# The MLP's first product by Strassen's scheme in three of four quarters of a one-core decoder block

## The chip, the cores and the metric

The kernel runs on one core of one Trainium2 chip. The metric is the device time of one execution in microseconds; the kernel before is given by the median of three runs. A profile of one further execution shows what each engine did: TensorE (PE, and PEld for its weight loads), VectorE (DVE), ScalarE (ACT), GpSimd (POOL) and SyncE (SP), whose queue issues the loads of weights.

## The reference, cut to what matters

```
x  is (512 tokens, 1024), w_mlp_in (1024, 4096), w_mlp_out (4096, 1024), all float32
x  = x + rmsnorm(merged @ w_out, g_post_mix)
h  = rmsnorm(x, g_pre_mlp)
f  = square(relu(h @ w_mlp_in)) @ w_mlp_out
x  = x + rmsnorm(f, g_post_mlp)
x  = x + sigmoid(x @ w_ple_gate) * (p @ w_ple_proj)
```

Ahead of this stand the three mixers (convolution, differential attention, pooling) with their gates; the change touches none of that.

## The kernel before

Activations lie with features on the partitions and the 512 tokens in the columns: a tile of 128 features is 128x512. All weights lie in one array of 144 chunks, 128x1024 each, in the order in which they are used; one chunk is one output tile of a 1024-deep product (eight blocks of 128x128, one for each step kt of the depth).

Each product keeps about float32 precision with the type float32r: both operands are split into a high and a low part, and `mm3` (lines 153 to 156) issues three matmuls for each block: high by high, weight high by moving low, weight low by moving high. A full output tile is 8 steps by 3 matmuls of 512 columns into one of eight PSUM banks (tags mm and at, four each; `bank2` takes them in turn).

`Weights` feeds this. `load` (L76) issues a chunk's DMA on SP's queue into one of three raw buffers. `split` makes the two parts: a cast on ScalarE (L90) into wh, then a subtraction on VectorE (L94) into wl. The parts go to slots; from the end of the mixers on there are eight (pools hlp with three and hlp2 with five), and `get` keeps the splits that many chunks ahead. A raw buffer is free when its subtraction has run.

The MLP is done in four quarters of 1024 hidden features. In each, eight output tiles of the first product (`one_tile(xg)`; xg is x1 times its gain, split, not yet normalised) go through `hidden`: VectorE takes max(b, 0) times rB2 (x1's rstd, L898), ScalarE squares (L899), and `mul_split` (L149 on ScalarE, L150 on VectorE) splits into sh and sl. Eight tiles of the second product (`one_tile(s_hl)`) follow and are added up in f: by a copy on ScalarE in quarter 0 (L934), by an addition on VectorE in quarters 1 and 2 (L936). In quarter 0 the first four output tiles are done side by side and in token halves of 256 (`side_by_side_halves`). In quarter 3 the second product runs in `split_output`: four tiles side by side, then four tiles in token halves, with TensorE's order written out by hand; `evac_f` (L907) adds to f, sums the squares for the next rmsnorm (L832, L835, L836) and scales (L909). Between the halves TensorE computes the rstd of a half (`rstd_steps`: L211 sums over partitions, VectorE and GpSimd take the power, L216 broadcasts), and `residual_half` (L853, L854) and a split make x2 for the last product.

Except where TensorE's order is written out by hand, a planner orders each engine's instructions ahead of time: of those that it takes to be ready it picks the one written first. On the chip each engine then runs its list strictly in that order.

Of the kernel before, what the change touches and what calls it, by code (L numbers as in the profile page):

```python
# [9 lines left out]
F32 = mybir.dt.float32  # L10
F32R = mybir.dt.float32r
AF = mybir.ActivationFunctionType
ALU = mybir.AluOpType
# [19 lines left out]
N_RAW, N_SPLIT, N_ACT, N_LOGIT, N_NORM, N_QK = 3, 3, 32, 6, 3, 12  # L33
TCARGS = dict(schedule_with_timeline_sim=True)
P = 128
S = 512
HALF = 256
D = 1024
# [9 lines left out]
G_PRE_MIX, G_POST_MIX, G_PRE_MLP, G_POST_MLP = 0, 8, 16, 24  # L48
# [9 lines left out]
class Weights:  # L58
# [3 lines left out]
    def __init__(self, tc, wdram, raw_pool, hl_pool):  # L62
        self.tc, self.nc, self.w = tc, tc.nc, wdram
        self.raw_pool = raw_pool
        self.turns = [hl_pool] * N_SPLIT
        self.n = wdram.shape[0]
        self.loaded = self.done = 0
        self.limit, self.pin = self.n, False
        self.tiles, self.raw = {}, {}

    def load(self, i, halves=False):
        while self.loaded <= min(i, self.n - 1):
            c = self.loaded
            self.raw[c] = self.raw_pool.tile([P, 1024], F32, tag="raw", name=f"raw{c}")
            if not halves:
                self.nc.sync.dma_start(out=self.raw[c], in_=self.w[c])  # L76
            self.loaded += 1
# [3 lines left out]
        self.nc.sync.dma_start(out=self.raw[c][:, sl], in_=self.w[c][:, sl])  # L81

    def tiles_of(self, c):
        pool = self.turns[c % len(self.turns)]
        return [pool.tile([P, 1024], F32R, tag=t, name=f"{t}{c}") for t in ("wh", "wl")]

    def split(self, c, sl=slice(0, 1024), parts="hl"):
        src, (wh, wl) = self.raw[c][:, sl], self.tiles[c]
        if "h" in parts:
            i = self.nc.scalar.copy(out=wh[:, sl], in_=src)  # L90
            if self.pin:
                self.tc.keep_in_program_order(i)
        if "l" in parts:
            i = self.nc.vector.tensor_tensor(out=wl[:, sl], in0=src, in1=wh[:, sl].bitcast(F32), op=ALU.subtract)  # L94
            if self.pin:
                self.tc.keep_in_program_order(i)

    def upto(self, i):
        while self.done <= min(i, self.n - 1):
            c = self.done  # L100
            self.load(c)
            self.tiles[c] = self.tiles_of(c)
            self.split(c)
            self.done += 1

    def get(self, i):
        self.upto(max(i, min(i + len(self.turns) - 1, self.limit)))
        return self.tiles[i]


# [1 line left out]
def block_kernel(ctx: ExitStack, tc: tile.TileContext, xT, pT, wts, pool_w, par, rel_bias, onehot, out):  # L112
    nc = tc.nc
# [20 lines left out]
    def act_tile(name, dt=F32, tag=None, pool=None, n=S):  # L134
        uid[0] += 1
        tag = tag or OWN.get(name, "a")
        return (pool or ap).tile([P, n], dt, tag=tag, name=f"{name}_{uid[0]}", bufs=BUFS.get(tag))

    def bank(tag="mm"):
        uid[0] += 1  # L140
# [12 lines left out]
    def mm3(o, sh, sl, mh, ml, first, last):  # L153
        nc.tensor.matmul(out=o, lhsT=sh, rhs=mh, start=first, stop=False)  # L154
        nc.tensor.matmul(out=o, lhsT=sh, rhs=ml, start=False, stop=False)  # L155
        nc.tensor.matmul(out=o, lhsT=sl, rhs=mh, start=False, stop=last)  # L156
# [37 lines left out]
    def pcol(c, n=1):  # L194
        return par_sb[:, c:c + n]
# [10 lines left out]
    def rstd_steps(sq, lo, n, inv_n, got, tag="at"):  # L206


        b = bank(tag)
        for j in range(n):  # L210
            nc.tensor.matmul(out=b[:, j:j + 1], lhsT=sq[:, lo + j * P:lo + (j + 1) * P], rhs=ones_col,  # L211
                             start=True, stop=True)
        r = rstd_from(b[:, 0:n], inv_n, n, "pe")
        yield
        for j in range(n):
            nc.tensor.transpose(out=b[:, j * P:(j + 1) * P], in_=r[:, j:j + 1].to_broadcast([P, P]), identity=ident)  # L216
        got(b[:, 0:n * P])
# [49 lines left out]
    chunk = [0]  # L267
# [484 lines left out]
        norm_g = Stream(conv_norm())  # L752
    drain(norm_g)
    atp_ctx.close()
    hlp2 = ctx.enter_context(tc.tile_pool(name="hlp2", bufs=8 - N_SPLIT))
    W.turns = [hlp] * N_SPLIT + [hlp2] * (8 - N_SPLIT)
    mg = []
    for m in range(KT):
        add_branch(m, conv_gates[m], y_mm(m, c_hl))
# [16 lines left out]
    def bank2():  # L776
        turn2[0] += 1
        return bank(("mm", "at")[turn2[0] % 2])
# [23 lines left out]
    def split_output(src, evac, done):  # L802

        W.limit = chunk[0] + KT + 3
        cs = [next_chunk() for _ in range(N_SIDE)]
        bs = [bank2() for _ in range(N_SIDE)]
        for kt in range(KT):
            for (wh, wl), b in zip(cs, bs):
                mm3(b, wh[:, kt * P:(kt + 1) * P], wl[:, kt * P:(kt + 1) * P], *src[kt], kt == 0, kt == KT - 1)
        for m in range(N_SIDE):  # L810
            evac(m, bs[m], slice(0, S))
        cs = [next_chunk() for _ in range(KT - N_SIDE)]
        bs = [bank2() for _ in range(KT - N_SIDE)]
        paced = None
        with tc.manual_schedule(engines={mybir.EngineType.PE}):
            for hf in range(2):
                for m in range(KT - N_SIDE):
                    for kt in range(KT):
                        half_mm(bs[m], *cs[m], src, kt, HALVES[hf], paced)
                    evac(m + N_SIDE, bs[m], HALVES[hf])  # L820
                if paced:
                    paced.finish()
                else:
                    paced = Paced(done(0), PACE_OUT)
# [5 lines left out]
    def sum_squares(total, src, first, sl):  # L830
        if first:
            nc.scalar.activation(out=total[:, sl], in_=src, func=AF.Square)  # L832
        else:
            q = act_tile("sq")
            nc.scalar.activation(out=q[:, sl], in_=src, func=AF.Square)  # L835
            nc.vector.tensor_tensor(out=total[:, sl], in0=total[:, sl], in1=q[:, sl], op=ALU.add)  # L836
# [29 lines left out]
    split_output(mg, evac_mix, mix_done)  # L866


    def side_by_side_halves(src, done):
        cs = [next_chunk() for _ in range(4)]  # L870
        bs = [bank2() for _ in range(4)]
        paced = Paced(done(1), PACE_IN)
        with tc.manual_schedule(engines={mybir.EngineType.PE}):
            for sl in HALVES:
                for kt in range(KT):
                    for c, b in zip(cs, bs):
                        half_mm(b, *c, src, kt, sl, paced)
                    if paced.n >= PACE_IN[1] + PACE_IN[2] * KT and W.limit < W.n:
                        W.limit, W.pin = W.n, True
                        W.upto(min(chunk[0] + W_AHEAD, W.n - 1))  # L880
                        W.pin = False
        paced.finish()
        return bs

    def one_tile(src):
        wh, wl = next_chunk()
        b = bank2()
        for kt in range(KT):
            mm3(b, wh[:, kt * P:(kt + 1) * P], wl[:, kt * P:(kt + 1) * P], *src[kt], kt == 0, kt == KT - 1)
        return b  # L890

    f = [act_tile("f", tag=t) for t in spare]
    fsum = act_tile("fsum", tag="norm")
    rB2 = [None]

    def hidden(b):
        t = act_tile("t")
        nc.vector.scalar_tensor_tensor(out=t, in0=b, scalar=0.0, in1=rB2[0], op0=ALU.max, op1=ALU.mult)  # L898
        nc.scalar.activation(out=t, in_=t, func=AF.Square)  # L899
        hl = act_tile("sh", F32R), act_tile("sl", F32R)  # L900
        mul_split(*hl, t)
        return hl
# [2 lines left out]

    def evac_f(m, b, sl):
        nc.vector.tensor_tensor(out=f[m][:, sl], in0=f[m][:, sl], in1=b[:, sl], op=ALU.add)  # L907
        sum_squares(fsum, f[m][:, sl], m == 0, sl)
        nc.scalar.activation(out=f[m][:, sl], in_=f[m][:, sl], func=AF.Copy, scale=pcol(G_POST_MLP + m))  # L909

# [8 lines left out]
    for quarter in range(4):  # L919
        s_hl = []  # L920
        if quarter == 0:
            bs = side_by_side_halves(xg, mix_done)
            rB2[0] = act_tile("rB")
            for _ in rstd_steps(x1sum, 0, 4, 1.0 / D, lambda b: nc.scalar.copy(out=rB2[0], in_=b)):
                pass
            s_hl = [hidden(b) for b in bs]
            s_hl += [hidden(one_tile(xg)) for _ in range(4)]
        else:
            s_hl = [hidden(one_tile(xg)) for _ in range(8)]
        if quarter < 3:  # L930
            for m in range(KT):
                b = one_tile(s_hl)
                if quarter == 0:
                    nc.scalar.copy(out=f[m], in_=b)  # L934
                else:
                    nc.vector.tensor_tensor(out=f[m], in0=f[m], in1=b, op=ALU.add)  # L936
        else:
            split_output(s_hl, evac_f, f_done)


# [137 lines left out]
```

## Time and profile before

| | |
|---|---|
| median of three runs | 838.5 us (837.84 to 839.13) |
| the profiled execution | 838.38 us, of which the span from first to last instruction is 836.6 us |
| busy: PE, PEld, DVE, ACT | 829.7, 699.8, 504.7, 347.1 us |
| granted TensorE clock | 0.999 of full |

Busy times are sums over the whole span. A PE instruction's shown duration is longer than the distance to the next one, because matmuls overlap; the distance from start to start is what a matmul costs in a stream. Back-to-back instructions on DVE and ACT overlap by a little too.

### The profile page before, as it was taken

The numbers are of one execution on the slowest core, as the hardware profiler recorded it, in microseconds if no ns is written. First come the engines' busy times: TensorE is split into PE (matmuls) and PEld (weight loads), VectorE is DVE, ScalarE is ACT, GpSimd is POOL, SyncE is SP. The second block draws the span as 40 slices with busy tenths as digits, with TensorE's granted clock in tenths as the row PEclk, the third lists the DMA queues.
The fourth block names the chain that finished last, engine by engine and source line by source line (L and its number), as shares of the span: only waits on it lengthen the run. The fifth ranks groups of instructions, "written<-read, shape, count | busy, mean of one in ns | idle before, by whom it ended". The sixth has DMA issues, their size and how long they took to land.

```text
span 836.6 us, 10573 instructions
## 1 busy us (share of the span) xinstructions
PE 829.7 (99%) x4132; PEld 699.8 (84%) x4132; DVE 504.7 (60%) x832; ACT 347.1 (41%) x560; POOL 29.0 (3%) x66
## 2 busy tenths in 40 slices
PE   8999999999999999999999999999999999999998
PEld 6788888888888888888999888888888888889997
DVE  5869669965579985675377631443334434435672
ACT  6734635555452323752445542342233223425341
POOL 2200000010000000000000000000000000000000
PEclk9999999999999999999999999999999999999999
DMA  8463332222222232265303423322223222223311
GB/s 281 153 229 108 113 101 76 86 80 75 77 75 82 95 101 88 92 219 181 101 2 119 158 80 122 101 95 85 98 101 100 98 83 97 100 76 99 104 61 67
DMA packets 27522, 89.09 MB, mean 106 GB/s; under 512 B 3244, under 2 KB 3628, under 8 KB 27472
## 3 DMA queue, kind: packets, MB, share of 16 engines
q1 hardware_dynamic: 26160, 83.95, 29.9%
q0 software_dynamic: 1312, 4.47, 1.5%
q8 instruction: 32, 0.52, 0.3%
q14 instruction: 18, 0.15, 0.1%
HBM read 84.20 MB, written 5.52 MB: 107 GB/s over the span
## 4 chain that ended last, share of the span: by engine, by line
PE 96%; DVE 2%; DMA 1%; ACT 1%; issue 0%; SPq 0%; DVEq 0%; ACTq 0%
PE mm L156 21%; PE mm L154 21%; PE mm L155 21%; PE at L154 10%; PE at L155 10%; PE at L156 10%; PE at L211 1%; DMA raw<-in_wts_dram 1%; PE at L457 1%; PE at L455 1%; PE at L488 1%; DVE ssum L294 1%; PE at L216 0%; DVE wl L94 0%; ACT wh L90 0%
## 5 line engine op out<-in xcount | busy, mean ns | idle before, releaser
L90 ACT CAST wh<-raw 128x1024 fp32r<-128x1024 f32 (+1 forms) x144 | 148.8, 1038 | 337.1 <-PE mm L155 147.1
L94 DVE TENSOR_TENSOR wl<-raw,wh 128x1024 fp32r<-128x1024 f32 (+1 forms) x144 | 173.4, 1208 | 105.3 <-ACT wh L90 105.1
L156 PE MATMUL mm<-xnh,wl 128*128 128x512 f32 x352 | 137.8, 392 | 0.5 <-DVE wl L94 0.4
L155 PE MATMUL mm<-xnl,wh 128*128 128x512 f32 x352 | 137.6, 391 | 0.0
L154 PE MATMUL mm<-xnh,wh 128*128 128x512 f32 x352 | 137.2, 393 | 0.0
L577 DVE SCALAR_TENSOR_TENSOR acc<-u,par_sb,acc 128x512 f32<-128x512 f32 x116 | 81.3, 744 | 1.2 <-ACT acc L571 1.1
L156 PEld LDWEIGHTS mm<-xnh,wl 128*128 128x128 f32 x352 | 66.1, 188 | 14.6 <-DVE wl L94 1.4
L154 PEld LDWEIGHTS mm<-xnh,wh 128*128 128x128 f32 x352 | 66.1, 188 | 14.2 <-ACT xnh L149 0.9
L155 PEld LDWEIGHTS mm<-xnl,wh 128*128 128x128 f32 x352 | 66.1, 188 | 14.1 <-DVE xnl L150 0.4
L154 PE MATMUL at<-sh,wh 128*128 128x512 f32 (+1 forms) x144 | 53.1, 369 | 0.0
L154 PE MATMUL mm<-sh,wh 128*128 128x512 f32 (+1 forms) x144 | 53.0, 368 | 0.0
L155 PE MATMUL mm<-sl,wh 128*128 128x512 f32 (+1 forms) x144 | 53.0, 368 | 0.0
L155 PE MATMUL at<-sl,wh 128*128 128x512 f32 (+1 forms) x144 | 52.9, 367 | 0.0
L156 PE MATMUL at<-sh,wl 128*128 128x512 f32 (+1 forms) x144 | 52.8, 367 | 0.0
L156 PE MATMUL mm<-sh,wl 128*128 128x512 f32 (+1 forms) x144 | 52.8, 367 | 0.0
L154 PE MATMUL at<-xgh,wh 128*128 128x512 f32 (+1 forms) x144 | 52.8, 367 | 0.0
L154 PE MATMUL mm<-xgh,wh 128*128 128x512 f32 (+1 forms) x144 | 52.8, 367 | 0.0
L155 PE MATMUL at<-xgl,wh 128*128 128x512 f32 (+1 forms) x144 | 52.7, 366 | 0.0
L156 PE MATMUL at<-xgh,wl 128*128 128x512 f32 (+1 forms) x144 | 52.7, 366 | 0.0
L155 PE MATMUL mm<-xgl,wh 128*128 128x512 f32 (+1 forms) x144 | 52.6, 365 | 0.0
L156 PE MATMUL mm<-xgh,wl 128*128 128x512 f32 (+1 forms) x144 | 52.6, 365 | 0.0
L898 DVE SCALAR_TENSOR_TENSOR t<-at,rB 128x512 f32<-128x512 f32 x16 | 11.0, 690 | 34.4 <-PE at L156 34.4
(251 smaller groups left out, 1521.8 us busy)
## 6 DMA issues: line engine op xcount, KB each, us to landing
raw<-in_wts_dram SPq DMA_DIRECT2D x140, 512.0 KB, 3.3
x<-in_xT_dram SPq DMA_DIRECT2D x16, 256.0 KB, 5.6
proj_d<-proj POOLq DMA_DIRECT2D x8, 256.0 KB, 4.0
proj<-proj_d SPq DMA_DIRECT2D x8, 256.0 KB, 3.2
out_dram<-pg SPq DMA_DIRECT2D x7, 256.0 KB, 2.1
rep_d<-rel_d POOLq DMA_DIRECT2D x4, 320.0 KB, 8.3
raw<-in_wts_dram SPq DMA_DIRECT2D x4, 256.0 KB, 5.8
bias<-rep_d POOLq DMA_DIRECT2D x4, 256.0 KB, 4.3
```

The costliest lines, as they stand in the source:

```text
L90: i = self.nc.scalar.copy(out=wh[:, sl], in_=src)
L94: i = self.nc.vector.tensor_tensor(out=wl[:, sl], in0=src, in1=wh[:, sl].bitcast(F32), op=ALU.subtract)
L154: nc.tensor.matmul(out=o, lhsT=sh, rhs=mh, start=first, stop=False)
L155: nc.tensor.matmul(out=o, lhsT=sh, rhs=ml, start=False, stop=False)
L156: nc.tensor.matmul(out=o, lhsT=sl, rhs=mh, start=False, stop=last)
L211: nc.tensor.matmul(out=b[:, j:j + 1], lhsT=sq[:, lo + j * P:lo + (j + 1) * P], rhs=ones_col, start=True, stop=True)
L294: nc.vector.tensor_tensor(out=ssum, in0=ssum, in1=q, op=ALU.add)
L455: nc.tensor.matmul(out=lg[m][:, 0:nn], lhsT=q[m][:, cols], rhs=k[m][:, 0:nn], start=True, stop=False)
L457: nc.tensor.matmul(out=lg[m][:, 0:nn], lhsT=ql[m][:, cols], rhs=k[m][:, 0:nn], start=False, stop=True)
L488: nc.tensor.transpose(out=tp[:, j * P:(j + 1) * P], in_=e[:, j * P:(j + 1) * P], identity=ident)
L577: nc.vector.scalar_tensor_tensor(out=t, in0=u[:, k:k + S], scalar=pcol(w0 + k), in1=t, op0=ALU.mult, op1=ALU.add)
L898: nc.vector.scalar_tensor_tensor(out=t, in0=b, scalar=0.0, in1=rB2[0], op0=ALU.max, op1=ALU.mult)
```

## The change

In quarters 1 to 3 two output tiles of the first product are computed together. Two weight chunks a and b form a 2x2 block matrix (the tile, by the depth 0 to 511 or 512 to 1023), xg a 2x2 block matrix (that depth, by the token half). Strassen's scheme in Winograd's form needs seven products of blocks in place of eight, and sums of blocks on both sides:

- `pair` and `split_sums`: for each pair the chunk list has three entries: w is the chunk a as before, s and r are sums of blocks. They are formed on VectorE in place in the raw buffers (four subtractions or additions of 512 columns), then split as a chunk is. The block b[:, R] (a22) is split too, into small tiles.
- `block_sums` forms the sums of xg's blocks, once, during quarter 0's second product: T2, T3 and T4 are kept in three of the eight slots (pool hlp3), a fourth replaces the right halves of xg[0..3]. So from the middle of quarter 0 to the end of quarter 3's pairs the weights have five slots.
- `tile_pair` does the seven products, each of four steps by three matmuls of 256 columns, into three banks (top, low, b), with VectorE and ScalarE adding the results up between them, in part in PSUM. Bank b's left half is used twice.
- `hidden`: ScalarE takes the relu (in VectorE's place), without rB2. rB2 becomes the square of x1's rstd, and `evac_f` multiplies f by it on VectorE, once for each part of f, in quarter 3.
- In quarter 0 the eight tiles are computed as before.

```diff
+    def pair(self, i):
+        self.items[i:i + 2] = [("w", i), ("s", i), ("r", i)]
+        self.n = len(self.items)
...
+    def split_sums(self, z, kind, c):
+        nc = self.nc
+        L, R = slice(0, 512), slice(512, 1024)
+        a, b = self.raw[c], self.raw[c + 1]
+        def sums(out, x, y, op=ALU.subtract):
+            nc.vector.tensor_tensor(out=out, in0=x, in1=y, op=op)
+        if kind == "s":
+            dh, dl = self.small_tile("a22h", F32R), self.small_tile("a22l", F32R)
+            nc.scalar.copy(out=dh, in_=b[:, R])
+            sums(dl, b[:, R], dh.bitcast(F32))
+            self.a22[z] = dh, dl
+            sums(b[:, R], b[:, L], b[:, R], ALU.add)
+            sums(b[:, L], a[:, L], b[:, L])
+            src = b
+        else:
+            sums(a[:, L], b[:, R], a[:, L])
+            sums(a[:, R], a[:, R], a[:, L])
+            src = a
+        h, l = self.tiles[z]
+        nc.scalar.copy(out=h, in_=src)
+        sums(l, src, h.bitcast(F32))
     def upto(self, i):
         while self.done <= min(i, self.n - 1):
-            c = self.done
-            self.load(c)
-            self.tiles[c] = self.tiles_of(c)
-            self.split(c)
+            z, (kind, c) = self.done, self.items[self.done]
+            self.load(c + (kind != "w"))
+            self.tiles[z] = self.tiles_of(z)
+            if kind == "w":
+                self.split(z)
+            else:
+                self.split_sums(z, kind, c)
             self.done += 1
     def get(self, i):
-        self.upto(max(i, min(i + len(self.turns) - 1, self.limit)))
+        self.upto(max(i, min(i + self.slots - 1, self.limit)))
         return self.tiles[i]
...
+    w1 = W.n - 72
+    for z in reversed(range(4, 16)):
+        W.pair(w1 + 16 * (z // 4) + 2 * (z % 4))
...
-    hlp2 = ctx.enter_context(tc.tile_pool(name="hlp2", bufs=8 - N_SPLIT))
-    W.turns = [hlp] * N_SPLIT + [hlp2] * (8 - N_SPLIT)
+    hlp2 = ctx.enter_context(tc.tile_pool(name="hlp2", bufs=2))
+    hlp3 = ctx.enter_context(tc.tile_pool(name="hlp3", bufs=3))
+    few = (hlp, N_SPLIT), (hlp2, 2)
+    W.pools(*few, (hlp3, 3))
...
+    def block_sums():
+        store = [[hlp3.tile([P, 1024], F32R, tag=t, name=f"T{n}{t}") for t in ("wh", "wl")] for n in range(3)]
+        def split(h, l, src):
+            nc.scalar.copy(out=h, in_=src)
+            nc.vector.tensor_tensor(out=l, in0=src, in1=h.bitcast(F32), op=ALU.subtract)
+        sub = lambda out, x, y: nc.vector.tensor_tensor(out=out, in0=x, in1=y, op=ALU.subtract)
+        for kt in range(4):
+            u, v = act_tile("u"), act_tile("v")
+            for t, m in ((u, kt), (v, kt + 4)):
+                nc.scalar.activation(out=t, in_=x_t[m], func=AF.Copy, scale=pcol(G_PRE_MLP + m))
+            sub(u[:, LO], u[:, HI], u[:, LO])
+            sub(u[:, HI], v[:, HI], u[:, HI])
+            sub(v[:, HI], v[:, HI], u[:, LO])
+            sub(v[:, LO], v[:, LO], v[:, HI])
+            split(*(t[:, HI] for t in xg[kt]), u[:, LO])
+            T[3, kt] = [t[:, kt * HALF:(kt + 1) * HALF] for t in store[0]]
+            split(*T[3, kt], u[:, HI])
+            yield
+            both = [t[:, kt % 2 * S:(kt % 2 + 1) * S] for t in store[1 + kt // 2]]
+            split(*both, v)
+            T[4, kt], T[2, kt] = ([t[:, sl] for t in both] for sl in HALVES)
+            yield
+    def tile_pair():
+        i = chunk[0]
+        W.upto(i + 4)
+        (ah, al), (sh, sl), (rh, rl) = (W.tiles[i + z] for z in range(3))
+        dh, dl = W.a22[i + 1]
+        chunk[0] += 3
+        top, low, b = bank2(), bank2(), bank2()
+        e = act_tile("e")
+        def product(o, wh, wl, w0, rhs):
+            for kt in range(4):
+                c0 = w0 + kt * P
+                mm3(o, wh[:, c0:c0 + P], wl[:, c0:c0 + P], *rhs(kt), kt == 0, kt == 3)
+        def x_block(k0, sl):
+            return lambda kt: [t[:, sl] for t in xg[k0 + kt]]
+        def t_block(n):
+            return lambda kt: T[n, kt]
+        add = lambda out, x, y: nc.vector.tensor_tensor(out=out, in0=x, in1=y, op=ALU.add)
+        u = act_tile("e")[:, LO]
+        product(b[:, LO], ah, al, 0, x_block(0, LO))
+        nc.scalar.copy(out=e[:, LO], in_=b[:, LO])
+        product(b[:, HI], rh, rl, 0, t_block(2))
+        add(u, b[:, HI], e[:, LO])
+        product(low[:, HI], sh, sl, 512, x_block(0, HI))
+        add(e[:, HI], low[:, HI], u)
+        product(top[:, LO], ah, al, 512, x_block(4, LO))
+        product(b[:, LO], sh, sl, 0, t_block(3))
+        add(u, b[:, LO], u)
+        product(top[:, HI], rh, rl, 512, x_block(4, HI))
+        add(top, top, e)
+        product(low[:, LO], dh, dl, 0, t_block(4))
+        both = low.rearrange("p (z q) -> p z q", q=HALF)
+        add(both, both, u[:, None, :].to_broadcast([P, 2, HALF]))
+        W.upto(min(i + 6, W.n - 1))
+        return [hidden(top), hidden(low)]
...
     def hidden(b):
         t = act_tile("t")
-        nc.vector.scalar_tensor_tensor(out=t, in0=b, scalar=0.0, in1=rB2[0], op0=ALU.max, op1=ALU.mult)
+        nc.scalar.activation(out=t, in_=b, func=AF.Relu)
         nc.scalar.activation(out=t, in_=t, func=AF.Square)
         hl = act_tile("sh", F32R), act_tile("sl", F32R)
...
     def evac_f(m, b, sl):
         nc.vector.tensor_tensor(out=f[m][:, sl], in0=f[m][:, sl], in1=b[:, sl], op=ALU.add)
+        nc.vector.tensor_tensor(out=f[m][:, sl], in0=f[m][:, sl], in1=rB2[0][:, sl], op=ALU.mult)
         sum_squares(fsum, f[m][:, sl], m == 0, sl)
...
             rB2[0] = act_tile("rB")
-            for _ in rstd_steps(x1sum, 0, 4, 1.0 / D, lambda b: nc.scalar.copy(out=rB2[0], in_=b)):
+            s_hl = [hidden(b) for b in bs]
+            for _ in rstd_steps(x1sum, 0, 4, 1.0 / D,
+                                lambda b: nc.scalar.activation(out=rB2[0], in_=b, func=AF.Square)):
                 pass
-            s_hl = [hidden(b) for b in bs]
+            W.pools(*few)
             s_hl += [hidden(one_tile(xg)) for _ in range(4)]
+            steps = block_sums()
         else:
-            s_hl = [hidden(one_tile(xg)) for _ in range(8)]
+            for _ in range(4):
+                s_hl += tile_pair()
         if quarter < 3:
             for m in range(KT):
                 b = one_tile(s_hl)
                 if quarter == 0:
                     nc.scalar.copy(out=f[m], in_=b)
+                    next(steps, None)
                 else:
                     nc.vector.tensor_tensor(out=f[m], in0=f[m], in1=b, op=ALU.add)
         else:
+            W.pools(*few, (hlp3, 3))
             split_output(s_hl, evac_f, f_done)
```

## Rows read from the trace of the kernel before

**Rows 1.** Page: busy us (share of the span) xinstructions of each engine.

```profile
PE 829.7 (99%) x4132; PEld 699.8 (84%) x4132; DVE 504.7 (60%) x832; ACT 347.1 (41%) x560; POOL 29.0 (3%) x66
```

**Rows 2.** Page: shares of the span, by engine, of the chain that ended last.

```profile
PE 96%; DVE 2%; DMA 1%; ACT 1%; issue 0%; SPq 0%; DVEq 0%; ACTq 0%
```

**Rows 3.** Timeline of DVE, the first `hidden` of quarters 1 and 3.

```profile
527.61 0.69 DVE L898 SCALAR_TENSOR_TENSOR t<-at,rB 128x512 f32<-128x512 f32 x1 [3.41 <-PE at L156]
...
703.26 0.69 DVE L898 SCALAR_TENSOR_TENSOR t<-at,rB 128x512 f32<-128x512 f32 x1 [3.40 <-PE at L156]
```

**Rows 4.** Timeline of PE: the 24 matmuls of one full tile, quarter 1.

```profile
560.05 0.39 PE L154 MATMUL mm<-xgh,wh 128*128 128x512 f32 x1
...
565.26 0.39 PE L156 MATMUL mm<-xgh,wl 128*128 128x512 f32 x1
565.49 0.39 PE L154 MATMUL at<-sh,wh 128*128 128x512 f32 x1
```

**Rows 5.** Timeline of PE: half-width matmuls, one bank (18), four banks in turn (27).

```profile
774.58 0.28 PE L154 MATMUL at<-sh,wh 128*128 128x256 f32 x1
...
776.59 0.28 PE L156 MATMUL at<-sh,wl 128*128 128x256 f32 x1
776.71 0.50 PE L211 MATMUL at<-ones_col,fsum 128*128 128x1 f32 x4
...
430.92 0.28 PE L154 MATMUL at<-xgh,wh 128*128 128x256 f32 x1
...
434.04 0.28 PE L156 MATMUL at<-xgh,wl 128*128 128x256 f32 x1
```

**Rows 6.** Stretches of half and full width: busy us by engine, PEclk, DMA share, GB/s.

```profile
431.00:455.50 24.50, 24.50 (x208) 24.50 (x207) 20.85 (x49) 13.41 (x32) 0.81 (x1) 1.00 0.18 60
...
530.00:560.00 30.00, 30.00 (x134) 24.86 (x133) 13.26 (x16) 11.10 (x15) 0.00 (x0) 1.00 0.32 105
```

**Rows 7.** Groups by line and shape: busy us, mean ns of one, idle before (us).

```profile
L94 DVE TENSOR_TENSOR wl<-raw,wh 128x1024 fp32r<-128x1024 f32 x140 | 170.6, 1223 | 99.2 <-ACT wh L90 99.1
L150 DVE SCALAR_TENSOR_TENSOR sl<-t,sh 128x512 fp32r<-128x512 f32 x32 | 22.2, 692 | 7.3 <-ACT sh L149 7.3
L853 DVE TENSOR_TENSOR f<-f,at 128x256 f32<-128x256 f32 x16 | 5.5, 415 | 2.0 <-PE at L216 2.0
...
L90 ACT CAST wh<-raw 128x1024 fp32r<-128x1024 f32 x140 | 146.4, 1050 | 332.8 <-PE mm L155 147.1 <-PE at L155 129.6 <-DMA raw<-in_wts_dram 25.9
L149 ACT ACTIVATE sh<-t 128x512 fp32r<-128x512 f32 x32 | 20.2, 633 | 1.0
L934 ACT COPY f<-at 128x512 f32<-128x512 f32 x4 | 2.3, 583 | 0.0
L835 ACT ACTIVATE sq<-mm 128x256 f32<-128x256 f32 x4 | 1.6, 405 | 4.9 <-PE mm L156 4.9
```

**Rows 8.** DMA issues: line, count, KB each, median us to landing.

```profile
raw<-in_wts_dram SPq DMA_DIRECT2D x140, 512.0 KB, 3.3
```

**Rows 9.** Timeline of DVE at the MLP's end; brackets: idle before, releaser.

```profile
761.34 0.69 DVE L907 TENSOR_TENSOR f<-f,at 128x512 f32<-128x512 f32 x1 [17.25 <-PE at L156]
...
769.10 0.42 DVE L907 TENSOR_TENSOR f<-f,mm 128x256 f32<-128x256 f32 x1 [0.23 <-PE mm L156]
...
771.93 0.42 DVE L907 TENSOR_TENSOR f<-f,at 128x256 f32<-128x256 f32 x1 [0.34 <-PE at L156]
...
774.77 0.42 DVE L907 TENSOR_TENSOR f<-f,mm 128x256 f32<-128x256 f32 x1 [1.51 <-PE mm L156]
775.68 0.43 DVE L836 TENSOR_TENSOR fsum<-fsum,sq 128x256 f32<-128x256 f32 x1 [0.49 <-ACT sq L835]
...
779.35 2.74 DVE L853 TENSOR_TENSOR f<-f,at 128x256 f32<-128x256 f32 x8
...
789.04 0.42 DVE L836 TENSOR_TENSOR fsum<-fsum,sq 128x256 f32<-128x256 f32 x1
```

**Rows 10.** The chain in order of time: start us, us; second half's sums.

```profile
790.00 0.34 PE at L211 x4
```

More of the change, by code (lines that the diff above doesn't have):

```diff
@@ L64, in __init__ @@
         self.raw_pool = raw_pool
-        self.turns = [hl_pool] * N_SPLIT
-        self.n = wdram.shape[0]
+        self.pools((hl_pool, N_SPLIT))
+        self.items = [("w", c) for c in range(wdram.shape[0])]
+        self.n = len(self.items)
+        self.a22 = {}
         self.loaded = self.done = 0
@@ L69, in __init__, with pools @@
         self.tiles, self.raw = {}, {}
+    def pools(self, *pools):
+        self.from_pools, self.slots = pools, sum(n for _, n in pools)
+        self.given = getattr(self, "given", {})
+    def pair(self, i):
+        self.items[i:i + 2] = [("w", i), ("s", i), ("r", i)]
+        self.n = len(self.items)
     def load(self, i, halves=False):
-        while self.loaded <= min(i, self.n - 1):
+        while self.loaded <= min(i, self.w.shape[0] - 1):
             c = self.loaded
@@ L83, in tiles_of, with oldest @@
     def tiles_of(self, c):
-        pool = self.turns[c % len(self.turns)]
+        def oldest(p):
+            past = self.given.setdefault(id(p[0]), [])
+            return past[-p[1]] if len(past) >= p[1] else -1
+        pool = min(self.from_pools, key=oldest)[0]
+        self.given[id(pool)].append(c)
         return [pool.tile([P, 1024], F32R, tag=t, name=f"{t}{c}") for t in ("wh", "wl")]
     def split(self, c, sl=slice(0, 1024), parts="hl"):
-        src, (wh, wl) = self.raw[c][:, sl], self.tiles[c]
+        src, (wh, wl) = self.raw[self.items[c][1]][:, sl], self.tiles[c]
         if "h" in parts:
@@ L137, in act_tile @@
         return (pool or ap).tile([P, n], dt, tag=tag, name=f"{name}_{uid[0]}", bufs=BUFS.get(tag))
+    W.small_tile = act_tile
+    w1 = W.n - 72
+    for z in reversed(range(4, 16)):
+        W.pair(w1 + 16 * (z // 4) + 2 * (z % 4))
     def bank(tag="mm"):
@@ L890, in one_tile @@
         return b
+    LO, HI = HALVES
+    T = {}
+    def block_sums():
[20 more added lines that the diff above has]
+            yield
```

## The prediction

> **What bounds the kernel now.** I read the page's busy shares first: TensorE is busy for 99% of the span, VectorE for 60%, ScalarE for 41% [rows 1]. The chain that ended last, by engine, says the same: 96% of it is TensorE, 2% VectorE, 1% DMA [rows 2]. So a matmul saved is time saved, as long as the engines that feed TensorE keep up. A busy share does not tell what a matmul costs, as matmuls overlap; for that I took the timeline of TensorE and the distance from one start to the next. A full tile (24 matmuls of 512 columns) takes from 560.05 to 565.49, 5.44 us, 0.2267 us each [rows 4]. Two quarters lie between the first `hidden` of quarter 1 and that of quarter 3: 175.65 us, 87.8 a quarter, and 16 tiles by 5.44 are 87.0 [rows 3]. TensorE streams through the MLP without gaps, at the full clock of 2.4 GHz (granted 1.00 in both stretches of [rows 6]).
>
> **The change: TensorE.** A pair of tiles costs 2 x 5.44 = 10.88 us now. Afterwards it is 7 products x 4 steps x 3 matmuls = 84 matmuls of 256 columns. The trace has that shape where token halves are done. Into one bank at a time, 17 distances between 774.58 and 776.59 make 0.1182 us each; into four banks in turn, 26 distances between 430.92 and 434.04 make 0.1200 [rows 5]. A half-width matmul so costs more than half of a full one (0.1133): the eighth that the scheme saves is partly eaten by 84 weight loads where there were 48. In the half-width stretch the weight loads are busy for all of 24.50 us, in the full-width one for 24.86 of 30 [rows 6]. The new products fill one bank at a time, but the planner may interleave two; I take 0.119. A pair is then 10.0 us and saves 0.88; twelve pairs save **10.6 us** (bounds 9.6 at 0.1200, 11.4 at 0.1182).
>
> The Trainium skill ("TensorE: Matmul & The Clock Gate", section "Back-to-back issue gap") gives the warm gap of a matmul by itself as N/2.4 + 2.5 ns, so by estimate 215.8 for 512 columns and 109.2 for 256. By it a pair would fall from 10.36 to 9.17 us and the twelve would save 14.2. The trace differs: both widths cost about 10 ns more here.
>
> **VectorE.** Per pair it gets three wl of 1.22 us (now two), the a22 part and four block sums of 512 columns (nearest row: L150, 0.69 each), three additions of 256 (0.415, a row that reads PSUM), two of 512 that write PSUM in place (no row writes PSUM from VectorE; I take 0.69), and two splits at 0.69 [rows 7]. That is 3.67 + 3.46 + 1.25 + 1.38 + 1.38 = 11.1 us against 10.0 of TensorE. Back to back, instructions overlap: eight of 256 columns take 2.74 [rows 9], 0.34 each and not 0.415, so 15 instructions may take 1.1 less, 10.0. Before, the same pair cost it 2 x (1.22 + 0.69 + 0.69) = 5.2. Over a quarter it is 4 x 11.1 + 8 x (1.22 + 0.69) = 60 of 83.5 us, so VectorE is not the bound on average; during the pairs it is level with TensorE, and what counts is when a split is wanted.
>
> ScalarE: three casts of 1.05, the a22 cast at about 0.6, the 256-column copy 0.4, and twice relu (0.58, as L934), square and cast (0.63 each): 7.8 of 10.0 us [rows 7]. Hidden behind TensorE; without that cover it would come onto the path of the last `hidden`, where the second product's first six depth steps (0.68 each) still give it 4 us.
>
> **The ring of raw buffers.** I count from the first product of pair 1. Five slots let w1, s1, r1 and w2 be split during the eight tiles before, where VectorE has 3.5 us free in each 5.44. r2 needs w1's slot, free after the fourth product, 5.7; with cast and subtraction it is done at 8.3 and wanted at 11.4, by pair 2's second product. Only then is a raw buffer free for pair 3's second chunk: 3.3 us to land [rows 8], 12.0 with the issue. s3 and r3 are 5 x 0.69 + 2 x 1.22 = 5.9 us of VectorE, and some 3 us of additions and splits of pairs 1 and 2 fall between: done at about 21, wanted at 21.4. The next turn takes as long again, 3.7 to load and 9 on VectorE: 33.7. r4 is wanted at 31.4 if the products keep the order in which they are written, at 34.4 if the planner puts the third and fourth product ahead of the second, which don't need it. So a quarter waits between 0 and 2.3 us here. The planner does put what is ready first, so I take the lower part, 0.7 a quarter: **+2.0 us** (bounds 0 and 6.9).
>
> **The MLP's end.** The multiplication by the squared rstd moves from `hidden` (where VectorE had time) to `evac_f`, in a stretch where TensorE's order is fixed. Ahead of the last addition of the first half (774.77) come four multiplications of 512 columns and three of 256: 3.5 to 4.0 us. VectorE's idle time there is 0.23 + 0.34 + 1.51 = 2.1. So that addition is 1.4 to 1.9 late; its own multiplication adds 0.4; fsum was ready at 776.11 and TensorE's sums over partitions started at 776.71 [rows 5, 9], so 0.6 is hidden: a wait of 1.2 to 1.7 us, and TensorE has behind it the halves still to do. In the second half fsum ends at 789.46 and its sums start at 790.00 [rows 9, 10]: four multiplications, 1.4 to 1.7, less 0.5, unless splits of x2 step back: 0 to 1.2. Together 0 (if splits of weights step back too) to 2.9; I take 1.5 + 0.5, **+2.0 us**.
>
> **At nothing.** `block_sums`: 4 x (6 subtractions of 256 and one of 512) = 4 x 3.2 = 13 us on VectorE and about as much on ScalarE, beside quarter 0's second product (43.5 us, in which VectorE has 8 wl, 9.8, besides). Without that cover, quarter 1 would start up to 3 us late. Five slots for eight: a chunk takes 3.3 + 1.05 + 1.22 = 5.6 us, one tile's time, so two slots ahead cover it. Quarter 0's `hidden` without rB2: one wait less on a chain off TensorE's path. The DMAs are as many and as large.
>
> **Sum.** The profiled execution took 838.4 us (span 836.6), the median of the runs 838.5. 838.4 - 10.6 + 2.0 + 2.0 = **831.8 us**.
>
> **The rivals.**
> A, the forecast: TensorE sets the pace, small waits. From 827 (saving 11.4, no wait) to 837.
>
> B, the shared bank. Bank b holds the first product on the left, then the second on the right, while ScalarE copies the left. If a write to one half has to wait for the reader of the other, the second product starts after the first one's last matmul has drained (0.28, of which 0.12 is the next start) and the copy (0.41): 0.16 + 0.41 + two hand-overs, 0.6 us. Twelve times 7.2, on top of the forecast: 839.0, no change. Against it: the third product goes to another bank and can fill the gap. For it: no row shows a bank shared so. The Trainium skill ("PSUM — Partial Sum Buffer", "PSUM bank collisions raise a hardware error") forbids two engines in one bank at a time, so the wait is to be expected; no run before shows its price.
>
> C, the other sign: the raw ring. If each turn takes 2 us more than above (VectorE idle in hand-overs, additions in front of the sums), r3 is ready at 23 and r4 at 37.5. Pair 3 then waits 0 to 1.6 and pair 4 3.1 to 6.1, about 5 us a quarter: 838.4 - 10.6 + 2.0 + 15 = 844.8. It turns slower than before from (10.6 - 2.0) / 3 = 2.9 us a quarter. For it: VectorE has 10 to 11 us of work per 10.0; against it: pairs 1 and 2 are prepared ahead, and only two turns are left in a quarter.
>
> D, half width costs exactly half, 0.1133: a pair 9.5, twelve save 16.3, 826.1. Against it stand all the half-width stretches. This is the direction of the skill's gap formula named above.
>
> E, the change saves no TensorE time: that needs 10.88 / 84 = 0.1295 us per half-width matmul, which no stretch shows: 842.4 with the waits of the forecast.
>
> **How the numbers follow.** A 62%, B 13%, C 17%, D 4%, E or a mishap of the same size 4%. The time is A's, 831.8, its own range 827 to 837. For 8 in 10 I take 828 to 843: above lie some two thirds of C, below it D and a little of A. A change of 0.2% (1.7 us) is what a measurement of this kernel can tell from none. Faster: A, D and a part of B, 0.74; the same: most of B, 0.09; slower: C and E, 0.17.
>
> **What would show it.** The distance between half-width matmuls in the pairs (0.118 to 0.120) and the time from pair to pair (10.0). VectorE nearly without idle time in the pairs. TensorE's waits: on the subtractions that end the splits of r and s (C), on the copy of bank b (B), at L211 in the MLP's end (1.5 and 0.5). The prediction is wrong if pairs 3 and 4 of a quarter take longer than pairs 1 and 2 by more than 3 us together, or if the end costs over 3.

## The result, and the profile after

The changed kernel takes 843.4 us (median of four, 841.63 to 843.57) against 838.2: ratio 1.006, interval 1.0046 to 1.0073. It is slower by about 5 us, where 831.8 was forecast. Its profiled execution has a span of 841.4 us against 836.6.

The page after, first part, and the chain by engine:

```profile
PE 824.9 (98%) x4564; PEld 715.4 (85%) x4564; DVE 577.3 (69%) x972; ACT 400.6 (48%) x648; POOL 29.1 (3%) x66
...
PE 92%; DVE 4%; DMA 1%; ACT 1%; issue 1%; SPq 0%; DVEq 0%; ACTq 0%
```

TensorE has 432 matmuls more, as 12 x (84 - 48) says, yet is busy for 4.8 us less; its share of the chain fell from 96% to 92%, and VectorE's rose from 2% to 4% [rows 1, 2]. So work was saved and waits came in. The view of waits, TensorE's, names them (us in total, times, longest):

```profile
PE at L207 <- ACT e L1004: 3.9, 3, 1.3
PE at L264 <- DVE fsum L892: 2.3, 2, 1.8
PE at L207 <- DVE e L1001: 2.1, 3, 0.9
PE mm L207 <- DVE e L1001: 1.8, 3, 0.6
```

L207 to L209 are `mm3` now, L264 the sums over partitions. L1004 is ScalarE's copy of the first product out of bank b's left half, L1001 the additions of VectorE. The waits come three to a quarter. In quarter 1, TensorE's timeline (the tiles T0wh and T0wl hold T3; T1 and T2 hold the halves of depth of T2 and T4 side by side):

```profile
542.00 0.28 PE L209 MATMUL mm<-T2wh,wl 128*128 128x256 f32 x1
542.87 0.39 PE L207 MATMUL mm<-T0wh,wh 128*128 128x256 f32 x1 [0.59 <-DVE e L1001]
...
551.47 0.28 PE L209 MATMUL mm<-xgh,wl 128*128 128x256 f32 x1
553.04 0.39 PE L207 MATMUL at<-T1wh,wh 128*128 128x256 f32 x1 [1.29 <-ACT e L1004]
```

The first pair of lines is the end of a second product and the start of the fifth: 0.87 us from start to start in place of 0.12. The second is the start of a second product, 1.57 after the matmul before it. A third gap, 0.87, follows at 554.45, and the matmul behind the first one after each gap starts 0.10 late too: 3.25 us in this quarter and in quarter 3, 3.6 in quarter 2, **10.1 in all**.

Why the copy was late stands in ScalarE's timeline, and the addition's time in VectorE's:

```profile
549.35 0.63 ACT L1027 ACTIVATE t<-t 128x512 f32<-128x512 f32 x1
550.02 0.63 ACT L202 ACTIVATE sh<-t 128x512 fp32r<-128x512 f32 x1
550.55 0.61 ACT L128 CAST a22h<-raw 128x512 fp32r<-128x512 f32 x1
551.67 1.04 ACT L109 CAST wh<-raw 128x1024 fp32r<-128x1024 f32 x1 [0.50 <-PE mm L208]
552.62 0.37 ACT L1004 COPY e<-at 128x256 f32<-128x256 f32 x1
```

```profile
542.39 0.43 DVE L1001 TENSOR_TENSOR e<-mm,e 128x256 f32<-128x256 f32 x1 [0.90 <-PE mm L209]
```

The copy stands behind a cast that itself waits for TensorE to release a slot. But it is later than that cast explains. It belongs to pair 3, whose top and b are banks of tag at; only the pair's first, fourth and sixth products bring blocks of xg there:

```profile
540.56 0.28 PE L209 MATMUL at<-xgh,wl 128*128 128x256 f32 x1
...
549.07 0.28 PE L209 MATMUL at<-xgh,wl 128*128 128x256 f32 x1
```

The first line ends the first and the fourth product (24 matmuls from 537.80 on), so the copy starts some 12 us after what it copies was done. The second line ends the sixth, which multiplies the same r as the second product: r was there, and the second product waited for the copy alone. The addition is not late: it starts when the second product has drained, 0.39 after its last matmul's start, and the fifth product starts 0.05 after the addition ends. In these waits no matmul into one half of bank b begins before the reader of the other half is done. That is what the Trainium skill ("PSUM — Partial Sum Buffer", "PSUM bank collisions raise a hardware error") asks of a kernel; the trace agrees, with these 0.05 us.

At the MLP's end (compare [rows 9]):

```profile
777.07 0.28 PE L209 MATMUL at<-sh,wl 128*128 128x256 f32 x1
779.14 0.61 PE L264 MATMUL at<-ones_col,fsum 128*128 128x1 f32 x4 [1.80 <-DVE fsum L892]
```

and the stretches behind it (length, PE, PEld, DVE, ACT, POOL busy, granted clock, DMA share, GB/s):

```profile
778.00:780.50 2.50, 1.36 (x11) 1.36 (x12) 1.04 (x4) 0.26 (x1) 0.47 (x1) 1.00 0.68 231
780.80:784.00 3.20, 3.20 (x18) 3.20 (x17) 1.94 (x6) 0.92 (x2) 0.00 (x0) 0.50 0.34 119
784.00:786.50 2.50, 2.50 (x22) 2.50 (x22) 2.50 (x9) 0.43 (x2) 0.00 (x0) 0.97 0.35 100
```

The sums of the first half start 2.08 after the matmul before them, where 0.12 is the rule. From 780.8 the granted clock is 0.50, the lower level (1.2 GHz), for 3.2 us; some 14 matmuls take 0.21 there and not 0.12, 1.4 us. The second half's sums wait 0.6 more. **4.0 us** for the end. With 0.80 saved per pair, -9.6 + 10.1 + 4.0 = +4.5, and the spans differ by 4.8.

### The profile page after: what moved, and what is told of

Read it like the earlier page. It is cut to its first block, busy times and chain, and to the rows that moved or that the text cites. A ratio compares the mean times of both kernels' runs of the same rounds, so it can differ in the third digit from the quotient of the medians.

```text
span 841.4 us, 11670 instructions
## 1 busy us (share of the span) xinstructions
PE 824.9 (98%) x4564; PEld 715.4 (85%) x4564; DVE 577.3 (69%) x972; ACT 400.6 (48%) x648; POOL 29.1 (3%) x66
## 4 chain that ended last, share of the span: by engine, by line
PE 92%; DVE 4%; DMA 1%; ACT 1%; issue 1%; SPq 0%; DVEq 0%; ACTq 0%
PE mm L207 20%; PE mm L209 20%; PE mm L208 20%; PE at L207 9%; PE at L208 9%; PE at L209 9%; DMA x<-in_xT_dram 1%; PE at L264 1%; ACT wh L109 1%; DVE wl L113 1%; PE at L510 1%; PE at L508 1%; DMA raw<-in_wts_dram 1%; DVE fsum L892 1%; PE at L541 1%
## 5 line engine op out<-in xcount | busy, mean ns | idle before, releaser
L109 ACT CAST wh<-raw 128x1024 fp32r<-128x1024 f32 (+1 forms) x132 | 135.7, 1038 | 215.0 <-PE mm L208 98.7
L113 DVE TENSOR_TENSOR wl<-raw,wh 128x1024 fp32r<-128x1024 f32 (+1 forms) x132 | 158.5, 1206 | 88.0 <-ACT wh L109 87.6
L209 PE MATMUL mm<-xnh,wl 128*128 128x512 f32 x352 | 137.9, 392 | 0.6 <-DVE wl L113 0.6
L207 PE MATMUL mm<-xnh,wh 128*128 128x512 f32 x352 | 137.3, 393 | 0.0
L209 PEld LDWEIGHTS mm<-xnh,wl 128*128 128x128 f32 x352 | 66.1, 188 | 14.7 <-DVE wl L113 1.5
L207 PEld LDWEIGHTS mm<-xnh,wh 128*128 128x128 f32 x352 | 66.1, 188 | 14.4 <-ACT xnh L202 0.9
L207 PE MATMUL mm<-sh,wh 128*128 128x512 f32 (+1 forms) x144 | 53.9, 374 | 0.0
L209 PE MATMUL mm<-sh,wl 128*128 128x512 f32 (+1 forms) x144 | 53.5, 372 | 0.0
L207 PE MATMUL at<-sh,wh 128*128 128x512 f32 (+1 forms) x144 | 53.2, 369 | 0.0
L209 PE MATMUL at<-sh,wl 128*128 128x512 f32 (+1 forms) x144 | 53.0, 368 | 0.0
L139 ACT CAST wh<-raw 128x1024 fp32r<-128x1024 f32 x24 | 25.2, 1051 | 46.0 <-DVE raw L124 26.1
L207 PE MATMUL at<-xgh,wh 128*128 128x256 f32 (+1 forms) x144 | 42.6, 296 | 0.0
L208 PE MATMUL at<-xgl,wh 128*128 128x256 f32 (+1 forms) x144 | 42.5, 295 | 0.0
L207 PE MATMUL mm<-xgh,wh 128*128 128x256 f32 (+1 forms) x144 | 42.5, 296 | 0.0
L209 PE MATMUL at<-xgh,wl 128*128 128x256 f32 (+1 forms) x144 | 42.5, 295 | 0.0
L208 PE MATMUL mm<-xgl,wh 128*128 128x256 f32 (+1 forms) x144 | 42.3, 295 | 0.0
L209 PE MATMUL mm<-xgh,wl 128*128 128x256 f32 (+1 forms) x144 | 41.9, 295 | 0.0
```

Of the source, the lines that this page charges most:

```text
L139: nc.scalar.copy(out=h, in_=src)
```

## The experiments

Two theories for the waits in the pairs were set against each other, the bank theory (a half of bank b can't be written while the other half is read) and the feeding theory (VectorE and ScalarE are late with r, s and copies, as in the prediction's ring). For the end they are the twelve multiplications, or splits of weights piling up behind the pairs. All ratios are to the kernel before.

**x1_banks.** A fourth bank for the second product.

```diff
-        top, low, b = bank2(), bank2(), bank2()
+        top, low, b, c = bank2(), bank2(), bank2(), bank2()
...
-        product(b[:, HI], rh, rl, 0, t_block(2))
-        add(u, b[:, HI], e[:, LO])
+        product(c[:, HI], rh, rl, 0, t_block(2))
+        add(u, c[:, HI], e[:, LO])
```

> Only one thing differs from the changed kernel: the second product (r by T2) goes to a fourth PSUM bank and no longer to the right half of bank b. Bank theory: the waits inside the pairs, 3.3 us in each of three quarters, come from one half of a bank having to wait for the reader of the other half; they go, and the time falls by about 9.9, from 843.4 to 833.5. Feeding theory: the waits come from VectorE and ScalarE being late with r, s and the copies; they only move to another product, and the time stays at 841 to 844.

Measured 830.6 us, 0.9914 (0.9899 to 0.9929): 12.8 us less than the changed kernel. TensorE's waits from the MLP on are only those for fsum:

```profile
PE at L264 <- DVE fsum L892: 1.6, 2, 1.2
```

Not one wait is left in twelve pairs. The end became cheaper as well, and the clock stayed full there; that is most of the difference to the 9.9 expected.

**x2_eps.** No multiplication of f: the last rmsnorm takes the squared rstd in as its epsilon.

```diff
+            nc.vector.scalar_tensor_tensor(out=c, in0=ssq, scalar=inv_n, in1=eps, op0=ALU.mult, op1=ALU.add)
...
-        nc.vector.tensor_tensor(out=f[m][:, sl], in0=f[m][:, sl], in1=rB2[0][:, sl], op=ALU.mult)
...
+            nc.vector.tensor_scalar(out=ms, in0=b[:, 0:4], scalar1=1.0 / D, scalar2=EPS, op0=ALU.mult, op1=ALU.add)
+            nc.vector.scalar_tensor_tensor(out=f_eps, in0=ms, scalar=EPS, in1=ms, op0=ALU.mult, op1=ALU.mult)
```

> The seven products as in the changed kernel, but f is never multiplied by the squared rstd: the last rmsnorm takes it in as its epsilon, EPS times (mean square of x1 plus EPS) squared, on a tile of 128x4. Theory of the multiplications: the end of the MLP lost 4.6 us (two waits for fsum of 2.0 and 0.6, the rest at the lower clock after the first) because of the twelve multiplications on VectorE; without them 843.4 - 4.6 = 838.8. Rival: VectorE is late there because splits of the last weights pile up behind the pairs; then the wait for fsum stays and the time is above 842.

Measured 838.2, 1.0001 (0.9992 to 1.0011), as the theory of the multiplications had it. The view of waits has no line for fsum any more; those of the pairs are as in the changed kernel.

**x3_both.** Both edits.

> The fourth bank and the epsilon together. If both theories hold, 843.4 - 9.9 - 4.6 = 828.9, which is the kernel before less 12 x 0.80 us for the matmuls saved. If the feeding theory holds instead of the bank theory, about 838.

Measured 828.6, 0.9888 (0.9873 to 0.9903): faster than the kernel before by 9.4 us. TensorE waits for nothing from the MLP on. That is the scheme's saving, 12 x 0.80 = 9.6, nearly whole.

**x4_no_pairs.** The kernel before with the multiplications at the end (rB2 squared for them, as in the change) and the relu on ScalarE, without pairs.

```diff
-        nc.vector.scalar_tensor_tensor(out=t, in0=b, scalar=0.0, in1=rB2[0], op0=ALU.max, op1=ALU.mult)
+        nc.scalar.activation(out=t, in_=b, func=AF.Relu)
...
+        nc.vector.tensor_tensor(out=f[m][:, sl], in0=f[m][:, sl], in1=rB2[0][:, sl], op=ALU.mult)
```

> The kernel before with the second part of the change alone: relu on ScalarE, no rB2 in hidden, and f multiplied by the squared rstd in the last quarter; no pairs. Theory of the multiplications: slower by the 4.6 us of the end, 842.8. Rival (pile-up of weight splits behind the pairs): VectorE has idle time ahead of the end here, so 838 to 839.5.

Measured 840.7, 1.0034 (1.002 to 1.0048): 2.7 us dearer, between the two expectations. The multiplications cost by themselves, but less than at the end of the changed kernel. Both waits for fsum:

```profile
775.62 0.28 PE L156 MATMUL at<-sh,wl 128*128 128x256 f32 x1
776.35 0.61 PE L211 MATMUL at<-ones_col,fsum 128*128 128x1 f32 x4 [0.45 <-DVE fsum L836]
...
789.45 0.28 PE L156 MATMUL at<-x2h,wl 128*128 128x256 f32 x1
790.92 0.58 PE L211 MATMUL at<-ones_col,fsum 128*128 128x1 f32 x4 [1.20 <-DVE fsum L836]
```

For the first half it is 0.73 from start to start here, 2.08 there; for the second 1.47 here, 0.76 there. Together that is 2.0 us above the stream here and 2.6 there, and the lower clock came on top only there. The rival, a pile of splits, is not what made the first wait longer: from its first addition to f to the last one to fsum for the first half VectorE takes 15.9 us here and 15.8 there, with four splits among it in both. But in the changed kernel it begins 13.8 us before TensorE's last matmul of the half (777.07), here 15.3 (775.62). First addition there, then here:

```profile
763.26 0.69 DVE L1035 TENSOR_TENSOR f<-f,at 128x512 f32<-128x512 f32 x1 [2.58 <-PE at L209]
...
760.36 0.69 DVE L907 TENSOR_TENSOR f<-f,at 128x512 f32<-128x512 f32 x1 [16.62 <-PE at L156]
```

VectorE waits for TensorE's first tile in both; why that tile comes nearer to the end in the changed kernel stays open.

**x5_half_width.** The kernel before, with the 24 first-product tiles of quarters 1 to 3 done in two halves.

```diff
+        for sl in HALVES:
+            for kt in range(KT):
+                half_mm(b, wh, wl, src, kt, sl, None)
```

> The kernel before, but the 24 tiles of the first product in quarters 1 to 3 are done in two token halves of 256 columns, one after the other into one bank; no pairs, no sums. It prices half width by itself. At 0.1200 us a half-width matmul (as in the pairs of the changed kernel) a tile costs 48 x 0.1200 = 5.76 and not 5.44: 24 x 0.32 = 7.7, so 845.7. At 0.119, as the prediction took it, 24 x 0.27 = 6.5, so 844.5; at 0.1182 (one bank at a time) 843.6.

Measured 845.4, 1.009 (1.0072 to 1.0107): 7.5 us for 24 tiles, 0.31 each. The half-width matmul costs 0.1200, into one bank at a time:

```profile
539.73 0.28 PE L154 MATMUL mm<-xgh,wh 128*128 128x256 f32 x1
...
540.93 0.28 PE L155 MATMUL mm<-xgl,wh 128*128 128x256 f32 x1
```

**x6_no_sums.** The changed kernel without the four block sums of weights for a pair.

```diff
-            sums(b[:, R], b[:, L], b[:, R], ALU.add)
-            sums(b[:, L], a[:, L], b[:, L])
...
-            sums(a[:, L], b[:, R], a[:, L])
-            sums(a[:, R], a[:, R], a[:, L])
```

> The changed kernel without the four sums of weight blocks for each pair (r and s are plain splits of the two chunks, so this part of the computation is left out and the result is not the reference's); banks and the multiplications of f as in the changed kernel. Feeding theory: with 2.8 us less on VectorE for each pair, r and s come in time, the waits in the pairs go, and the time falls by about 10, to 833. Bank theory: every hand-over of a bank half is still there; the waits stay or shrink by less than half, 839 to 843.

Measured 841.1, 1.0036 (1.0023 to 1.0049). By the time the bank theory is met, but not by its waits:

```profile
PE mm L205 <- DVE wl L113: 4.9, 5, 1.4
PE at L260 <- DVE fsum L888: 4.0, 2, 3.8
```

With VectorE relieved, no hand-over of bank b costs anything, though the bank is shared as before. One wait of 1.7 us a quarter for a plain weight split (the split of w, L113) stands in their place, and the end is worse, a gap of 4.09 us and over 5 us at the lower clock:

```profile
776.50:781.60 5.10, 5.10 (x25) 5.10 (x25) 2.58 (x8) 0.93 (x2) 0.70 (x1) 0.50 0.49 140
```

Between the second product of pair 2 and its fifth (T0), 18 matmuls of the next pairs stand here (L203 to L205 are `mm3` in this run):

```profile
543.64 0.28 PE L203 MATMUL at<-xgh,wh 128*128 128x256 f32 x1
...
545.80 0.28 PE L203 MATMUL mm<-T0wh,wh 128*128 128x256 f32 x1
```

When a pair's r is ready can be read from the subtraction that ends its split. The start of pair 1 and r of pairs 3 and 4 in the changed kernel, then the same in x1, then the start of pair 1 and r of pair 4 in x6:

```profile
521.99 0.28 PE L207 MATMUL at<-xgh,wh 128*128 128x256 f32 x1
545.72 1.22 DVE L124 TENSOR_TENSOR wl<-raw,wh 128x1024 fp32r<-128x1024 f32 x1
558.77 1.22 DVE L124 TENSOR_TENSOR wl<-raw,wh 128x1024 fp32r<-128x1024 f32 x1
...
522.64 0.28 PE L207 MATMUL at<-xgh,wh 128*128 128x256 f32 x1
545.25 1.22 DVE L124 TENSOR_TENSOR wl<-raw,wh 128x1024 fp32r<-128x1024 f32 x1
558.67 1.22 DVE L124 TENSOR_TENSOR wl<-raw,wh 128x1024 fp32r<-128x1024 f32 x1
...
521.35 0.28 PE L203 MATMUL at<-xgh,wh 128*128 128x256 f32 x1
544.80 1.22 DVE L124 TENSOR_TENSOR wl<-raw,wh 128x1024 fp32r<-128x1024 f32 x1
```

Counted to the end of the subtraction, r of pair 4 comes 38.0 us after the start of pair 1 in the changed kernel, 37.2 in x1 and 24.7 in x6; r of pair 3 comes after 25.0 and 23.8. So x1 has the lateness without the shared bank, x6 the shared bank without the lateness, and neither has the waits. A hand-over costs where nothing else is ready to fill it: in the changed kernel the next pair's s and r are not yet split then (r of pair 3 at 546.94, after the gap at 542.00; r of pair 4 at 559.99, after those at 551.47 and 554.45). Both theories had half of it.

**x7_fifth_apart.** A fourth bank, but for the fifth product.

```diff
-        top, low, b = bank2(), bank2(), bank2()
+        top, low, b, c = bank2(), bank2(), bank2(), bank2()
...
-        product(b[:, LO], sh, sl, 0, t_block(3))
-        add(u, b[:, LO], u)
+        product(c[:, LO], sh, sl, 0, t_block(3))
+        add(u, c[:, LO], u)
```

> The changed kernel with a fourth bank for the fifth product (s by T3) and not for the second: the second product still has to wait for ScalarE's copy of bank b's left half, the fifth no longer for VectorE's addition from the right half. Bank theory: of the 3.3 us a quarter the two waits on the addition go (0.85 each) and the wait on the copy stays (1.55): 843.4 - 3 x 1.7 = 838.3. Feeding theory: no change, 842 to 844.

Measured 847.2, 1.0107 (1.0091 to 1.0122): slower than the changed kernel by 4, which neither theory expected. The fifth product no longer waits, the copy still costs 0.6 to 0.9, and a new wait of 3 us a quarter appears: the first tile of the second product wants a bank that an addition has not yet read out. The end is dearer too: a gap of 3.54 us there came with the lower clock.

```profile
553.70 0.28 PE L209 MATMUL at<-T2wh,wl 128*128 128x256 f32 x1
556.89 0.50 PE L207 MATMUL at<-sh,wh 128*128 128x512 f32 x1 [2.90 <-DVE e L1001]
```

The addition stands in VectorE's queue behind a subtraction (L113) whose cast waits for a load:

```profile
551.87 0.36 ACT L1004 COPY e<-at 128x256 f32<-128x256 f32 x1
553.59 1.04 ACT L109 CAST wh<-raw 128x1024 fp32r<-128x1024 f32 x1 [1.36 <-DMA raw<-in_wts_dram]
```

```profile
554.67 1.22 DVE L113 TENSOR_TENSOR wl<-raw,wh 128x1024 fp32r<-128x1024 f32 x1 [1.17 <-ACT wh L109]
555.81 0.68 DVE L124 TENSOR_TENSOR raw<-raw,raw 128x512 f32<-128x512 f32 x1
556.42 0.42 DVE L1001 TENSOR_TENSOR e<-at,e 128x256 f32<-128x256 f32 x1
```

**x8_relu_vector.** The version with both edits, its relu on VectorE.

```diff
-        nc.scalar.activation(out=t, in_=b, func=AF.Relu)
+        nc.vector.tensor_scalar(out=t, in0=b, scalar1=0.0, scalar2=None, op0=ALU.max)
```

> The version with both cures (828.6), but the relu of every tile is done by VectorE (0.69 us) instead of ScalarE: 1.4 us more for each pair. If VectorE is at its limit in the pairs, as the prediction's sum of 10.0 to 11.1 us of work for each 10.0 us says, TensorE waits by up to 2 us a pair from the second pair on, 8 to 15 us in all: 837 to 844. If there is room, because what is split ahead of the pairs and what can be put off covers it, the time stays below 830.5.

Measured 832.0, 0.9925 (0.991 to 0.994): 3.4 us more than with ScalarE's relu, between the two. VectorE gets eight relus of 0.68 us, 5.5, more in each quarter's pairs, and TensorE waits 1.0 to 1.4 a quarter, in the second products of the third and the fourth pair, for the cast that splits r. There is room, but less than 5.5 us of it.

**x9_order** and **x10_order_eps.** Three banks as in the changed kernel, the products written in the order 1, 4, 3, 2, 6, 5, 7; x10 also has the epsilon.

```diff
         product(b[:, LO], ah, al, 0, x_block(0, LO))
         nc.scalar.copy(out=e[:, LO], in_=b[:, LO])
+        product(top[:, LO], ah, al, 512, x_block(4, LO))
+        product(low[:, HI], sh, sl, 512, x_block(0, HI))
         product(b[:, HI], rh, rl, 0, t_block(2))
         add(u, b[:, HI], e[:, LO])
-        product(low[:, HI], sh, sl, 512, x_block(0, HI))
         add(e[:, HI], low[:, HI], u)
-        product(top[:, LO], ah, al, 512, x_block(4, LO))
+        product(top[:, HI], rh, rl, 512, x_block(4, HI))
         product(b[:, LO], sh, sl, 0, t_block(3))
         add(u, b[:, LO], u)
-        product(top[:, HI], rh, rl, 512, x_block(4, HI))
```

> The changed kernel with three banks as it is, but the seven products written in another order: 1, 4, 3, 2, 6, 5, 7, so that between each use of a half of bank b and the next use of the other half stands at least one product of 1.44 us in another bank. Hand-over theory: the waits need both a shared bank and two of its products back to back; 1.44 us cover the addition (0.42 and its start) and mostly the copy, so most of the 3.3 us a quarter go: 834 to 837, with the end as dear as before. Queue theory: the copy and the additions are late because they stand in a strict queue behind casts and subtractions that wait for a slot or a load; then another product waits for them, and the time stays above 840.

> The same order of products, and the epsilon in place of the multiplications of f. Hand-over theory: 829 to 831, close to the version with the fourth bank and the epsilon (828.6). Queue theory: 835 or more.

Measured 845.2, 1.008 (1.0064 to 1.0097), and 841.6, 1.0043 (1.0029 to 1.0056): no cure, 2 and 3.4 us slower than without the new order. The waits of x10:

```profile
PE at L207 <- ACT e L1007: 5.4, 3, 1.8
PE at L207 <- DVE e L1004: 2.6, 3, 1.2
```

The same two kinds of wait (the copy, now L1007, and the addition, L1004), fewer and longer: from start to start its six gaps take 9.3 us above the stream, and the nine of x2, which has the first order, 9.0. Most of what x10 is slower by stands in the clock, which fell to the lower level behind these gaps in two quarters:

```profile
554.20:560.80 6.60, 6.01 (x29) 5.72 (x28) 6.06 (x11) 4.59 (x6) 0.00 (x0) 0.50 0.22 78
731.70:738.30 6.60, 5.74 (x26) 5.45 (x26) 6.50 (x11) 3.75 (x5) 0.00 (x0) 0.50 0.29 95
```

With 1.000 granted over a whole execution x10 took 839.3. The planner's list put the copy behind a split and two casts again, in spite of the new order. The queue theory holds here.

## Why the prediction was wrong

**What bounds the kernel**: right. TensorE's work and waits account for the whole change.

**TensorE's saving**: the term 10.6 is 9.6, its lower bound. The price of 0.1200 holds for the products of xg's blocks in all pairs and in x5 (0.119 to 0.120 for those of the sums); that one bank at a time gives 0.1182 was read from a stretch of the second product and did not carry over, so the number of banks was not what told those stretches apart.

**VectorE's work**: 60 us a quarter were forecast; over 88 us it is busy for 29.1 + 27.0 = 56.1, the overlap taken off. "Level with TensorE in the pairs" was too strong: it is busy for 29 of the first 40 us, since splits are done ahead and behind:

```profile
523.00:563.00 40.00, 37.53 (x298) 36.39 (x298) 29.10 (x41) 22.56 (x33) 0.00 (x0) 1.00 0.30 94
563.00:611.00 48.00, 48.00 (x236) 40.14 (x235) 27.00 (x36) 16.81 (x21) 0.00 (x0) 1.00 0.31 98
```

**The ring, +2.0: the step that failed.** It asked when r and s are done and let the planner fill the time with the third and fourth products. The waits are 10.1, and none of the large ones is for r or s themselves. The ring did turn more slowly than forecast, 25.0 and 38.0 us for r of pairs 3 and 4 where 21 and 33.7 were put; but with 23.8 and 37.2 x1 waits for nothing, so this lateness costs nothing alone. Rival B had the place (bank b, second product after the copy) and was set aside with the same argument, that the third product can fill the gap. It could not: when the late copy let the second product start, the pair's first, third, fourth and sixth were done and the next pair's s and r not yet split. The second and fifth stood alone, and each use of a bank half waited for the reader of the other. Nor was B's size right: not 0.6 in each of twelve pairs, but nine waits of 0.85 to 1.55. The copy's wait was sized at its drain and duration; what it cost was its place in a strict queue. x1 shows that the shared bank is needed for these waits, x6 that without the sums they vanish too. That the earlier s and r are what does it in x6 is argued, as its whole list of instructions is another one; and why the planner put the copy so late was not tested. Rival C had the ring's times nearly right (23 and 37.5), and its 844.8 is near the measured 843.4 by luck: TensorE's waits for the split of r, from which it was added up, are not in the changed kernel. They appear in x8.

**The MLP's end, +2.0**: the mechanism was right, and the sum where TensorE does not wait elsewhere: 2.7 in x4, 830.6 - 828.6 = 2.0 between x1 and x3. That it fits is in part luck, as 1.5 and 0.5 were put for the two halves and x4 shows 0.6 and 1.35. In the changed kernel it was 4.0, above the 3 that the prediction named as a sign of being wrong. Two parts were missing from the term: VectorE began with f 1.5 us nearer to the end of TensorE's work, and the first wait took the clock down, 1.4 us.

**At nothing**: right. In x3, with block sums beside quarter 0 and five slots, TensorE waits for nothing.

**Rival E and D**: no stretch at the full clock came near 0.1295 or 0.1133. The chance for slower, 0.17, is too low for the prediction's own rivals: C and E have 17% and 4%, 0.21.

## What to carry to other kernels

Two accumulations in two halves of one PSUM bank were one resource here: each hand-over from a reader to the next product was a wait on TensorE whenever nothing else was ready, and the cover must be counted at the moment of the hand-over, from what is split by then, not on average. A small copy that releases TensorE costs its place in a strict queue, not its duration. The cure that held was a bank for the product behind the copy (x1), not one for another product (x7) and not another written order (x9, x10). Look for an algebraic home for a broadcast factor before paying VectorE for it at the one place where it has no time: here the factor fits into the epsilon of the next norm.

## What the runs showed of the hardware that was not expected

The lower clock did not follow from the length of a wait alone. A gap of 2.08 us at the end of the changed kernel was followed by 3.2 us at 0.50; gaps of 3.1 to 3.2 us in the three quarters of x7 were not followed by a slower pace, and one of 3.54 at its end came with the lower clock; in x10 two of three quarters with gaps of 2.09 and about 1.0 to 1.4 had it. Full and half-width matmuls in the first product fit one fixed part: 0.2267 and 0.1200 us at 2.4 GHz are 512 + 32 and 256 + 32 columns' time (worked out from the two distances), so two half-width matmuls cost 0.0133 us more than a full one.
